# Dealing the rows of a repeated RMSNorm to partitions in sixteen groups of eight

## The chip, the core and the metric

The kernel runs on one core of a Trainium2 chip. The metric is the device time of one execution in microseconds (us), lower is better. The kernel before was timed three times: 238.52, 238.64 and 238.80 us, median 238.64 us.

## What is computed

The input x has 8 x 512 rows of 2,048 float32 numbers, 4,096 rows and 33.6 MB in all. Each row is written out twice, one copy after the other, and each copy is divided by the root of its mean square and multiplied by gamma. The output has 8,192 rows, 67.1 MB.

```python
def reference(x, gamma):
    B, S, D = x.shape
    x_rep = np.repeat(x, 2, axis=1)
    rms = np.sqrt((x_rep ** 2).mean(axis=-1, keepdims=True) + 1e-6)
    x_norm = x_rep / rms
    return (x_norm * gamma[None, None, :]).astype(np.float32)
```

Every row is treated by itself, so the row that a partition works on can be any row, as long as its two results are written where that row's results belong.

## The kernel before

The 4,096 rows are cut into four blocks of 1,024. In a block, SBUF partition p holds eight neighbouring rows: rows 8p to 8p + 7 of the block, 8 x 8,192 = 65,536 bytes in one piece. A block is brought in by one load (`load`, line 50): 128 partitions of 65,536 bytes, 8.39 MB. Its results, 16 rows for each partition, leave in two stores (`store`, line 53): h = 0 takes the results of the partition's first four rows, h = 1 those of the last four. Each store also moves 128 pieces of 65,536 bytes, 8.39 MB. So the kernel issues four loads and eight stores, all of one size, and all on the queue of SyncE (SP). In DRAM, the pieces of a load lie end to end (piece p + 1 begins where piece p ends); those of a store begin 131,072 bytes apart, because the other half's results lie between them.

All rows are held in one SBUF tensor `y` of 24 rows per partition, seen as three thirds of eight rows: `first`, `second` and `third`. The function `four` handles two blocks and is called twice (lines 128 and 129). It loads block n into the upper half of `first` and the lower half of `second` (line 92), and block n + 1 into `third` (line 94). Then, for each half block, ScalarE (ACT) squares the rows and sums them (`squares`, line 63) and takes the root of the mean (line 67); VectorE (DVE) forms the reciprocal (line 73) and multiplies each row by it and by gamma (`scale`, line 75); ScalarE or VectorE copies each result row to the row behind it (`repeat`, line 82); and the half is stored. Stores follow at lines 99, 103, 108 and 111.

The order of the work is written by hand. The SP queue works through loads and stores in the order in which they stand: two loads, four stores, and the same again in the second call. A load of the second call waits until the stores that read the same thirds have landed; each store waits for the copies that fill its third.

The two views of DRAM that the change touches are made at the top:

```python
    x_t = x.rearrange("b s d -> (b s) d").rearrange("(n p k) d -> n p k d", p=P, k=H * K)
    out_t = out.rearrange("b s d -> (b s) d").rearrange("(n p h j) d -> n h p (j d)", p=P, h=H, j=K * R)
```

P is 128, H is 2, K is 4 and R is 2. Gamma comes in by two small transfers on ScalarE's queue and is spread over the partitions by GpSimd (POOL).

Of the kernel before, what the change touches and what calls it, by code (L numbers as in the profile page):

```python
# [1 line left out]

# [4 lines left out]


@with_exitstack
def kernel(  # L10
    ctx: ExitStack,
    tc: tile.TileContext,
    x: bass.AP,
    gamma: bass.AP,
    out: bass.AP,
):
    nc = tc.nc
    P = nc.NUM_PARTITIONS
    f32 = mybir.dt.float32
    Act = mybir.ActivationFunctionType  # L20
    Alu = mybir.AluOpType

    B, S, D = x.shape
    Bo, So, Do = out.shape
    R = So // S
    assert R == 2 and D == Do and B == Bo and So == S * R
    eps = 1e-6
    inv_d = 1.0 / float(D)


    K = 4
    N = B * S
    ntiles = N // (P * K)
    assert N % (P * K) == 0 and ntiles == 8
    H = 2
    x_t = x.rearrange("b s d -> (b s) d").rearrange("(n p k) d -> n p k d", p=P, k=H * K)
    out_t = out.rearrange("b s d -> (b s) d").rearrange("(n p h j) d -> n h p (j d)", p=P, h=H, j=K * R)

    singles = ctx.enter_context(tc.tile_pool(name="singles", bufs=1))
    rows = ctx.enter_context(tc.tile_pool(name="rows", bufs=1))  # L40
    junk = ctx.enter_context(tc.tile_pool(name="junk", bufs=1, space=bass.MemoryType.PSUM))
    small = ctx.enter_context(tc.tile_pool(name="small", bufs=4))

    y = rows.tile([P, 3 * K * R, D], f32, name="y")
    first, second, third = 0, K * R, 2 * K * R

    def load(n, at):
        nc.sync.dma_start(out=y[:, at : at + H * K, :], in_=x_t[n])  # L50

    def store(n, h, to):
        nc.sync.dma_start(
            out=out_t[n, h], in_=y[:, to : to + K * R, :].rearrange("p j d -> p (j d)")
        )

    def squares(at, rows):

        n = len(rows)
        ss = small.tile([P, n], f32, name=f"ss{n}")  # L60
        for c, k in enumerate(rows):
            sq = junk.tile([P, D], f32, name="sq")
            nc.scalar.activation(  # L63
                out=sq[:], in_=y[:, at + k, :], func=Act.Square, accum_out=ss[:, c : c + 1]
            )
        rms = small.tile([P, n], f32, name=f"rms{n}")
        nc.scalar.activation(out=rms[:], in_=ss[:], func=Act.Sqrt, scale=inv_d, bias=eps_t[:])  # L67
        return rms

    def scale(at, to, rows, rms):  # L70
        n = len(rows)
        rstd = small.tile([P, n], f32, name=f"rstd{n}")
        nc.vector.reciprocal(out=rstd[:], in_=rms[:])  # L73
        for c, k in enumerate(rows):
            nc.vector.scalar_tensor_tensor(  # L75
                out=y[:, to + R * k, :], in0=y[:, at + k, :], scalar=rstd[:, c : c + 1],
                in1=gamma_b[:], op0=Alu.mult, op1=Alu.mult,
            )

    def repeat(to, k0, k1, copy):  # L80
        y_r = y[:, to + R * k0 : to + R * k1, :].rearrange("p (k r) d -> p k r d", r=R)
        copy(out=y_r[:, :, 1, :], in_=y_r[:, :, 0, :])  # L82

    ctx.enter_context(tc.manual_schedule())

    half = K // 2
    up, down = list(range(K)), list(range(K - 1, -1, -1))

    def four(n, constants):


        load(n, first + K)
        constants()
        load(n + 1, third)
        for rows in (up[:half], up[half:]):
            scale(first + K, first, rows, squares(first + K, rows))
        repeat(first, 0, half, nc.scalar.copy)
        repeat(first, half, K, nc.vector.tensor_copy)
        store(n, 0, first)
        scale(second, second, down, squares(second, down))  # L100
        repeat(second, half, K, nc.scalar.copy)
        repeat(second, 0, half, nc.vector.tensor_copy)
        store(n, 1, second)
        roots = [squares(third + h * K, up) for h in range(H)]
        scale(third, first, up, roots[0])
        repeat(first, 0, half, nc.scalar.copy)
        repeat(first, half, K, nc.scalar.copy)
        store(n + 1, 0, first)
        scale(third + K, third, up, roots[1])
        repeat(third, 0, K, nc.scalar.copy)  # L110
        store(n + 1, 1, third)

    gamma_b = singles.tile([P, D], f32, name="gamma_b")
    eps_t = singles.tile([P, 1], f32, name="eps_t")

    def constants():
        for c0 in (0, D // 2):
            nc.scalar.dma_start(
                out=gamma_b[0:1, c0 : c0 + D // 2],
                in_=gamma[c0 : c0 + D // 2].partition_broadcast(1),  # L120
            )
        nc.gpsimd.partition_broadcast(out_ap=gamma_b[:], in_ap=gamma_b[0:1, :])  # L122
        nc.vector.memset(eps_t, eps)  # L123

        root = singles.tile([P, 1], f32, name="root")
        nc.scalar.activation(out=root[:], in_=eps_t[:], func=Act.Sqrt)  # L126

    four(0, constants)
    four(2, lambda: None)


# [1 line left out]
_INS = ['x', 'gamma']  # L133
_OUTS = [((8, 1024, 2048), 'float32')]


# [23 lines left out]
```

## Time and profile before

| | |
|---|---|
| profiled execution, its own time | 238.68 us |
| its span (first to last record) | 236.7 us |
| median of the three timed runs | 238.64 us |
| ACT busy | 110.2 us, 47% of the span |
| DVE busy | 84.4 us, 36% |
| POOL busy | 2.5 us, 1% |
| moved by DMA | 100.68 MB in 1,733 packets, mean 425 GB/s |
| the SP queue's packets (q1) | 1,728: 1,536 of 65,536 bytes, and 192 that signal an end |
| one issue on the SP queue | 0.33 to 0.43 us |
| a load, from issue to landing | 39.2 us median |
| a store, from issue to landing | 24.8 us median |

A transfer is cut into packets, which sixteen DMA engines carry. The profile gives each packet's start, duration, size and queue, but not which of the sixteen engines carried it, nor which partition or address it served. The time from issue to landing contains the time in which a transfer stands behind earlier ones on the same sixteen engines. The duration of a single packet of 65,536 bytes in this execution is 2,418 ns in the median.

### The profile page before, as it was taken

What the parts mean: (1) busy time and instruction counts of PE and PEld (TensorE: products, weight loads), DVE (VectorE), ACT (ScalarE), POOL (GpSimd) and SP (SyncE); (2) the same over time, 40 slices, a digit from 0 to 9 for tenths busy, and PEclk for the clock granted to TensorE, in tenths of its full rate; (3) what the DMA queues carried; (4) which work ended last, traced back from release to release, by engine and by line L of the source; (5) the groups of instructions that cost most, each with busy time, mean ns of one, the idle gap of its engine ahead of it and who ended that gap; (6) DMA issues with size and microseconds to landing.
All of it is one profiled execution on the core that took longest, in us unless ns stands there. A gap on an engine that the chain in (4) does not pass through costs nothing.

```text
span 236.7 us, 218 instructions
## 1 busy us (share of the span) xinstructions
DVE 84.4 (36%) x47; ACT 110.2 (47%) x86; POOL 2.5 (1%) x5
## 2 busy tenths in 40 slices
DVE  0000495594699400000000008929909992000000
ACT  2001989479998460000000058991999947300000
POOL 0210000000000000000000000000000000000000
DMA  9898989999898989899898989899898989899894
GB/s 355 355 532 354 532 354 487 399 443 443 365 520 354 532 354 509 377 465 421 354 532 354 532 354 520 367 399 487 354 532 354 520 365 509 376 465 421 365 520 177
DMA packets 1733, 100.68 MB, mean 425 GB/s; under 512 B 194, under 2 KB 194, under 8 KB 196
## 3 DMA queue, kind: packets, MB, share of 16 engines
q1 hardware_dynamic: 1728, 100.66, 98.5%
q10 hardware_dynamic: 4, 0.01, 0.0%
q14 instruction: 1, 0.01, 0.0%
HBM read 33.56 MB, written 67.11 MB: 425 GB/s over the span
## 4 chain that ended last, share of the span: by engine, by line
DMA 45%; ACT 26%; DVE 13%; issue 1%; DVEq 0%; SPq 0%
DMA y<-in_x_dram 26%; DMA out_dram<-y 20%; ACT sq L63 15%; DVE y L75 13%; ACT y L82 11%; ACT rms L67 1%; DVE rstd L73 0%; DVEq L75 0%; SPq L50 0%
## 5 line engine op out<-in xcount | busy, mean ns | idle before, releaser
L63 ACT ACTIVATE sq<-y 128x2048 f32<-128x2048 f32 x32 | 60.1, 1878 | 72.0 <-DMA y<-in_x_dram 71.3
L75 DVE SCALAR_TENSOR_TENSOR y<-y,rstd,gamma_b 128x2048 f32<-128x2048 f32 x32 | 73.8, 2349 | 2.1 <-DMA out_dram<-y 1.5
L82 ACT COPY y<-y 128x4096 f32<-128x4096 f32 (+1 forms) x10 | 42.6, 4283 | 19.5 <-DVE y L75 19.5
L73 DVE RECIPROCAL rstd<-rms 128x4 f32<-128x4 f32 (+1 forms) x10 | 1.7, 170 | 109.0 <-ACT rms L67 109.0
L82 DVE COPY y<-y 128x4096 f32<-128x4096 f32 x4 | 9.2, 2293 | 0.1
L63 ACT ACTIVATION_READ_ACCUMULATOR sq<-y 128x1 f32 x32 | 6.0, 186 | 0.0
L67 ACT ACTIVATE rms<-ss,eps_t 128x4 f32<-128x4 f32 (+1 forms) x10 | 3.0, 297 | 0.3
L122 POOL PARTITION_BROADCAST gamma_b<-gamma_b x1 | 2.3, 2294 | 10.2 <-DMA gamma_b<-in_gamma_dram 10.2
L126 ACT ACT_TABLE_LOAD x1 | 1.3, 1283 | 1.5 <-PEq L144 1.5
L123 DVE MEMSET eps_t<- 128x1 f32 x1 | 0.1, 59 | 0.8 <-PEq L144 0.8
L126 ACT ACTIVATE root<-eps_t 128x1 f32<-128x1 f32 x1 | 0.2, 203 | 0.0
L144 POOL MEMSET const-bfloat16-1.0<- 128x1 bf16 x1 | 0.1, 103 | 0.0
L144 POOL MEMSET const-float32-0.0<- 128x1 f32 x1 | 0.1, 100 | 0.2 <-issue 0.2
L144 POOL MEMSET const-uint8-127<- 128x1 uint8 x1 | 0.1, 102 | 0.0
L144 POOL MEMSET const-float32-1.0<- 128x1 f32 x1 | 0.1, 99 | 0.0
## 6 DMA issues: line engine op xcount, KB each, us to landing
out_dram<-y SPq DMA_DIRECT2D x8, 24.8
y<-in_x_dram SPq DMA_DIRECT2D x4, 39.2
gamma_b<-in_gamma_dram ACTq DMA_DIRECT2D x2, 4.0 KB
```

The costliest lines, as they stand in the source:

```text
L63: nc.scalar.activation(out=sq[:], in_=y[:, at + k, :], func=Act.Square, accum_out=ss[:, c : c + 1])
L67: nc.scalar.activation(out=rms[:], in_=ss[:], func=Act.Sqrt, scale=inv_d, bias=eps_t[:])
L73: nc.vector.reciprocal(out=rstd[:], in_=rms[:])
L75: nc.vector.scalar_tensor_tensor(out=y[:, to + R * k, :], in0=y[:, at + k, :], scalar=rstd[:, c : c + 1], in1=gamma_b[:], op0=Alu.mult, op ...
L82: copy(out=y_r[:, :, 1, :], in_=y_r[:, :, 0, :])
L122: nc.gpsimd.partition_broadcast(out_ap=gamma_b[:], in_ap=gamma_b[0:1, :])
L123: nc.vector.memset(eps_t, eps)
L126: nc.scalar.activation(out=root[:], in_=eps_t[:], func=Act.Sqrt)
L144: nc = _bacc.Bacc("TRN2", target_bir_lowering=False, num_devices=1)
```

## The change

Both DRAM views are cut another way. The 128 partitions are thought of as sixteen groups (`e`) of eight (`r`), partition p = 8e + r. Before, partition p held piece p of the block. After, it holds piece 16r + e. So the eight partitions of one group hold pieces that are sixteen pieces apart, and the first partitions of the sixteen groups hold sixteen pieces that lie next to each other. The DRAM side of every load and store now counts in three dimensions, 16 groups, 8 pieces, 16,384 numbers, where it counted 128 pieces before; the SBUF side still counts 128 partitions of 16,384 numbers. The new helper `groups` names this SBUF side for both. Number, size and order of the transfers stay the same, and so do all instructions of ACT and DVE and all SBUF addresses.

```diff
-    x_t = x.rearrange("b s d -> (b s) d").rearrange("(n p k) d -> n p k d", p=P, k=H * K)
-    out_t = out.rearrange("b s d -> (b s) d").rearrange("(n p h j) d -> n h p (j d)", p=P, h=H, j=K * R)
+
+    E = 16
+    x_t = x.rearrange("b s d -> (b s) d").rearrange(
+        "(n r e k) d -> n e r (k d)", r=P // E, e=E, k=H * K
+    )
+    out_t = out.rearrange("b s d -> (b s) d").rearrange(
+        "(n r e h j) d -> n h e r (j d)", r=P // E, e=E, h=H, j=K * R
+    )
...
+    def groups(at):
+        return y[:, at : at + K * R, :].rearrange("p j d -> p (j d)")
+
     def load(n, at):
-        nc.sync.dma_start(out=y[:, at : at + H * K, :], in_=x_t[n])
+        nc.sync.dma_start(out=groups(at), in_=x_t[n])
 
     def store(n, h, to):
-        nc.sync.dma_start(
-            out=out_t[n, h], in_=y[:, to : to + K * R, :].rearrange("p j d -> p (j d)")
-        )
+        nc.sync.dma_start(out=out_t[n, h], in_=groups(to))
```

## The prediction

> **What bounds the kernel now.** I read the busy shares first, then the page's table of DMA queues, then its forty slices, then a table of equal stretches of time, and the chain of waits last.
>
> ```profile
> span 236.7 us, 218 instructions
> DVE 84.4 (36%) x47; ACT 110.2 (47%) x86; POOL 2.5 (1%) x5
> ...
> DMA  9898989999898989899898989899898989899894
> GB/s 355 355 532 354 532 354 487 399 443 443 365 520 354 532 354 509 377 465 421 354 532 354 532 354 520 367 399 487 354 532 354 520 365 509 376 465 421 365 520 177
> ...
> q1 hardware_dynamic: 1728, 100.66, 98.5%
> ...
> DMA y<-in_x_dram 26%; DMA out_dram<-y 20%; ACT sq L63 15%; DVE y L75 13%; ACT y L82 11%; ACT rms L67 1%; DVE rstd L73 0%; DVEq L75 0%; SPq L50 0%
> ```
>
> No compute engine is busy half of the time. The sixteen DMA engines are: the SP queue alone fills 98.5% of their span, 0.985 x 236.7 = 233.1 us for each. The swing between 354 and 532 GB/s is one of counting: a slice lasts 5.92 us, and 2 or 3 rounds of sixteen 65,536-byte packets (1.05 MB) end in it. The chain names compute for some 40% of the span, but that is work done while the queue still held earlier transfers; I don't price by it.
>
> Next, whether loads and stores run at one rate. Each transfer takes about 19.35 us, so stretches of 38.7 us hold two:
>
> ```profile
> core 0: us, DVE busy (x) ACT busy (x) POOL busy (x), PEclk, DMA share, GB/s
> 1.70:40.40 38.70, 11.85 (x7) 18.20 (x18) 2.29 (x1) 1.00 1.02 434
> 40.40:79.10 38.70, 29.52 (x16) 30.41 (x26) 0.00 (x0) 1.00 1.00 434
> 79.10:117.80 38.70, 0.81 (x1) 7.02 (x1) 0.00 (x0) 1.00 1.01 434
> 117.80:156.50 38.70, 11.85 (x7) 17.00 (x16) 0.00 (x0) 1.00 1.00 434
> ```
>
> The first stretch is two loads, the second two stores, and both move 434 GB/s, whatever ACT and DVE do beside them. A limit that differs between reading and writing DRAM would show here. What both directions share is the DMA engine and its way to SBUF. The packet records agree: of the 1,536 packets of 65,536 bytes all but 38 last within 22 ns of 2.418 us (27.1 GB/s each). The exceptions are fifteen in the first round (2.5 to 3.4 us), sixteen around 117 us, where the queue passes from stores to loads, and a few strays; together they exceed the floor by 0.96 us per engine. A lone 4,096-byte packet of gamma takes 0.156 us, 26 GB/s: one engine alone is as fast as one among sixteen. So the row reads as sixteen separate ways, each full, not as one shared total.
>
> The sum of the profiled execution: 1,536 / 16 = 96 packets x 2.418 = 232.1 us per engine; 0.96 us above the floor; 0.6 us of gaps between first and last packet; 3.0 us of span before and after; 2.0 us outside the span (238.68 against 236.7). That makes 238.7; the median of the runs is 238.64, so no correction is due.
>
> **The change, part by part.** It removes and adds no instruction: four loads and eight stores stay on the SP queue, at 0.33 to 0.43 us an issue, hidden behind the transfers already queued; a third counting dimension could lengthen these twelve issues, and while a transfer of 19.35 us stands in the queue that costs nothing (if the first issue alone doubled, 0.4 us would show). Squares, scales and copies read and write the same SBUF addresses with the same shapes: difference nothing. Were their cover gone, ACT's 110.2 us would have to show; it lies beside 233.1 us of transfers.
>
> Two things do move. One is the DRAM address at which the sixteen engines work at a time. Its most favourable price is the removal of all that stands above the floor: -0.96 us, and no more, since 1,498 packets already stand on 2.418. Its least favourable one is the first round's mean, about 3.05 us, for every packet: 96 x 0.63 = +60 us. I take 0, because 1,498 of the 1,536 rows are at the floor with either direction's address pattern.
>
> [...]
>
> The other is the dealing of partitions to engines. Before, both sides of a transfer counted 128; now DRAM counts 16 x 8 and SBUF 128. If each engine takes one of the sixteen, it serves eight neighbouring partitions, one after the other, and all engines step through their groups together. The trace of before shows neither which engine serves which partitions nor how the ways into SBUF are shared, so this is bounded from both sides. Below: every engine keeps a way of its own, 0 us. Above: engines meet in pairs, and two packets share what one had, 2 x 2.418 = 4.84 us a packet and +232.1 us on the whole. The ends lie far apart. The nearest rows are the two 434 GB/s stretches, which say that a way has nothing to spare: whatever sharing comes in is paid in full. I take sharing in pairs, less what the engines' offset saves. The sixteen end signals of one transfer come within 0.4 to 1.0 us, first to last, so two engines of a pair are 0.1 to 1.0 us apart. If they share a way for half a group (my assumption: four packets, 9.67 us at the floor) and then move on together, the earlier one is alone for that offset: 1% to 10% of the sharing goes, 209 to 230 us stay. At 5%: 0.95 x 232.1 = +220.5 us.
>
> [...]
>
> What is late next: all transfers stretch alike, so the waits of loads on stores and of stores on copies become shorter in proportion; ACT's and DVE's work, which fitted beside transfers of 19.35 us, fits beside longer ones. Gamma's second piece, late behind the first load's packets, is needed only after that load has landed. No new wait is added.
>
> **Sum.** 238.7 + 220.5 + 0 = 459 us.
>
> **Rivals.**
>
> 1. *Each engine keeps its own way* (the regrouping leaves the dealing of partitions as it was, or the ways aren't shared; then the change does to DRAM addresses alone what it says, or not even that). For it: 1,498 packets at one duration in both directions, and no sign of sharing anywhere. Against it: the two sides no longer count alike. Price -0.96 to +0.5 us: 237.7 to 239.2 us. Within it, the faster end needs half of the slow first rounds to go: 238.2 or less. This rival is the one that isn't slower.
>
> 2. *Pairs meet once and part.* If one engine of a pair is favoured, it gets four packets ahead, the other follows on the way that it left, and both are full from there. One wait of 4 x 2.418 = 9.7 us, 248 us; with a slow parting anything up to the forecast, so 248 to 400. For it: the spacing of the end signals repeats from transfer to transfer, so an offset once gained persists. Against: nothing in the rows favours an engine.
>
> 3. *DRAM decides.* Neighbouring pieces at a time collide, and packets last as in the first round: on the loads alone a third of 60 us, 259 us; on all, 299 us. For it: the slow rounds stand at the first load's start and where stores give way to loads. Against: they are over within two rounds, though the address pattern goes on.
>
> **How the numbers follow.** Forecast 0.58, rival 1 0.27, rival 2 0.10, rival 3 0.05. The forecast's own range is 400 to 472 us: up to full sharing (238.7 + 232.1 = 471) and a little, down to where a third of the sharing is gone. What the measurement can tell from no change is 0.2%, 0.48 us. Rival 1 splits into 0.16 faster and 0.11 within 0.2%. Slower has the rest, 0.73. To hold the time 8 times in 10 the range must reach from the forecast over rivals 2 and 3 to the unchanged part of rival 1: 238.1 to 474 us, which leaves out the faster 0.16 and a small tail. The cases of both signs are so far apart that nothing narrower would be honest.
>
> **What would show it.** Right: packets of 65,536 bytes near 4.8 us with some at 2.418 where a pair is apart; the SP queue's share still above 95%; the rate in a stretch near 220 GB/s for loads and stores alike; a transfer near 37 us; busy times of ACT and DVE as before. Rival 1: packets at 2.418 us, and only the first rounds differ. Rival 2: long packets at the start only. Rival 3: loads and stores at different rates. The forecast is wrong if loads stay near 434 GB/s in the first 40 us.

## The result, and the profile after

| | before | after |
|---|---|---|
| median | 238.68 us (4 runs, 238.52 to 238.80) | 450.86 us (4 runs, 447.69 to 452.09) |
| profiled execution, its span | 238.68 us, 236.7 us | 447.69 us, 445.6 us |
| a load, from issue to landing, median | 39.2 us | 79.7 us |
| a store, the same | 24.8 us | 73.1 us |

The changed kernel takes 1.886 times as long (95% interval 1.880 to 1.892). The forecast was 459 us, 1.9% above the median.

The page of the changed kernel, in the order in which the page of before was read (span, busy engines, DMA share and rate in forty slices, the SP queue):

```profile
span 445.6 us, 216 instructions
...
DVE 84.4 (19%) x47; ACT 110.8 (25%) x86; POOL 2.5 (1%) x5
...
DMA  9999999989999998999999999998999899999930
GB/s 189 212 259 188 188 188 212 353 188 200 241 218 224 229 224 224 218 247 277 194 253 224 224 200 212 224 229 300 282 265 300 224 253 282 224 247 247 253 100 24
...
q1 hardware_dynamic: 1728, 100.66, 95.9%
```

ACT and DVE are busy for as long as before, within 0.6 us. The number and the bytes of the packets are the same. The DMA engines are busy almost throughout, as before, and move half as much: the queue's share of 95.9% goes with a mean of 226 GB/s here, 98.5% went with 425 before. So a busy DMA share says that packets are under way, not that they are fast. Two stretches of 36 us, one in each of the first two loads (columns: window, its length, busy time of DVE, ACT and POOL, PE clock, DMA share, GB/s):

```profile
5.00:41.00 36.00, 0.00 (x0) 0.00 (x0) 2.29 (x1) 1.00 0.99 204
44.00:80.00 36.00, 23.55 (x13) 23.91 (x21) 0.00 (x0) 1.00 0.99 204
```

204 GB/s stand where 434 stood. The packet records say the same by single packets: 5.12 us in the median of the first load, 2.12 times the 2.418 us of before. Later in the run the rate is more often 220 to 300 GB/s, and there packets of all durations from 2.4 to 6.0 us occur. The end signals of the sixteen engines, which lie within 1.1 us in the two first loads, lie 12 us apart at the second call's first load and 25.5 us apart in the last store: engines drift apart. The last two slices of the DMA row (3 and 0 tenths) are the tail in which only some of them still have work.

The parts of the 447.7 us: 232.1 at the floor, 194.9 per engine above it, 15.1 of gaps (most of them that tail), and 5.6 around the transfers. Before, these were 232.1, 0.96, 0.64 and 5.0.

### The profile page after: what moved, and what is told of

Its sections match the earlier page's. It is cut to its first block, busy times and chain, and to the rows that moved or that the text cites. A ratio compares the mean times of both kernels' runs of the same rounds, so it can differ in the third digit from the quotient of the medians.

```text
span 445.6 us, 216 instructions
## 1 busy us (share of the span) xinstructions
DVE 84.4 (19%) x47; ACT 110.8 (25%) x86; POOL 2.5 (1%) x5
## 3 DMA queue, kind: packets, MB, share of 16 engines
q1 hardware_dynamic: 1728, 100.66, 95.9%
## 4 chain that ended last, share of the span: by engine, by line
another core or an unknown queue 44%; ACT 16%; DVE 13%; DMA 10%; issue 0%; DVEq 0%
DVE y L82 12%; DMA y<-in_x_dram 10%; ACT sq L70 9%; ACT y L89 6%; ACT rms L74 0%; DVE rstd L80 0%; DVEq L82 0%
## 5 line engine op out<-in xcount | busy, mean ns | idle before, releaser
L70 ACT ACTIVATE sq<-y 128x2048 f32<-128x2048 f32 x32 | 60.1, 1878 | 188.6 <-DMA y<-in_x_dram 187.9
L82 DVE SCALAR_TENSOR_TENSOR y<-y,rstd,gamma_b 128x2048 f32<-128x2048 f32 x32 | 73.8, 2348 | 49.9 <-DMA out_dram<-y 49.4
## 6 DMA issues: line engine op xcount, KB each, us to landing
out_dram<-y SPq DMA_DIRECT2D x8, 73.1
y<-in_x_dram SPq DMA_DIRECT2D x4, 79.7
```

Source lines behind the costliest of these rows:

```text
L70: nc.scalar.activation(out=sq[:], in_=y[:, at + k, :], func=Act.Square, accum_out=ss[:, c : c + 1])
L82: nc.vector.scalar_tensor_tensor(out=y[:, to + R * k, :], in0=y[:, at + k, :], scalar=rstd[:, c : c + 1], in1=gamma_b[:], op0=Alu.mult, op ...
```

## The experiments

Three theories were set against each other. *Dealing*: each engine serves one group of eight neighbouring partitions, and engines whose partitions lie 32 apart share a way into SBUF. *DRAM*: neighbouring runs, read or written at one time, collide. *The count*: a DRAM side in three dimensions costs by itself. All times below are medians, against the kernel before on the same chip (238.6 to 238.8 us).

### The same groups, far apart in DRAM

```diff
-        "(n r e k) d -> n e r (k d)", r=P // E, e=E, k=H * K
+        "(e n r k) d -> n e r (k d)", r=P // E, e=E, k=H * K
...
-        "(n r e h j) d -> n h e r (j d)", r=P // E, e=E, h=H, j=K * R
+        "(e n r h j) d -> n h e r (j d)", r=P // E, e=E, h=H, j=K * R
```

> Sixteen groups of eight as in the change, but each group's eight pieces lie end to end in DRAM and the groups 2 MiB apart (block n takes pieces 32e + 8n + r), so that no two engines are at neighbouring runs. Dealing theory (each engine serves eight neighbouring partitions and pairs of engines share a way into SBUF, wherever the DRAM addresses are): 440 to 460 us, packets again near 5.1 us in the first loads. DRAM theory (neighbouring runs at the same time collide): back near 239 us, packets 2.42 us.

Measured: 444.3 us in the median; three runs took 444.3 to 445.5 us, and one took 431.97, below the expectation. So 193 to 207 of the 212 us of loss are there. The packets of the first loads last 5.12 us again, and 5 to 41 us into the run 204 GB/s are moved, as in the changed kernel. Nothing is neighbouring here. The DRAM theory falls as the cause.

### 128 on both sides, other addresses

```diff
-    x_t = x.rearrange("b s d -> (b s) d").rearrange("(n p k) d -> n p k d", p=P, k=H * K)
+    x_t = x.rearrange("b s d -> (b s) d").rearrange("(p n k) d -> n p k d", p=P, k=H * K)
...
-    ... "(n p h j) d -> n h p (j d)" ...
+    ... "(p n h j) d -> n h p (j d)" ...
```

> DRAM is counted by 128 on both sides as before, but the blocks are interleaved: partition p of block n holds piece 4p + n, so pieces lie 256 KiB apart in a load and 512 KiB in a store instead of 64 and 128. Dealing theory: addresses don't matter, 238.2 to 239.5 us. DRAM theory: another address pattern gives another time, more than 2% away from 238.7.

Measured: 240.55 us, 1.0079 (1.0064 to 1.0094). That is between the two expectations: addresses do matter, by 1.9 us, but that is less than a hundredth of what the change cost. The packet records place the loss: 2.28 us per engine above the floor instead of 0.96, and the excess lies where stores give way to the loads of the second call, 110 to 130 us into the run.

### The loads alone, the stores alone

The edits are against the changed kernel. For the loads alone, `out_t` goes back to the count of before:

```diff
-        "(n r e h j) d -> n h e r (j d)", r=P // E, e=E, h=H, j=K * R
+        "(n p h j) d -> n h p (j d)", p=P, h=H, j=K * R
```

For the stores alone, `x_t` does:

```diff
-        "(n r e k) d -> n e r (k d)", r=P // E, e=E, k=H * K
+        "(n p k) d -> n p (k d)", p=P, k=H * K
```

> Only the loads are dealt in sixteen groups of eight; the stores keep the view of before, so the output rows stand in another order than the reference's. Dealing theory: four of twelve transfers take 5.12 instead of 2.42 us a packet: 4 x 8 x 2.70 = 86 us more, about 325 us, less what pairs that part save (from 300). If only writing to DRAM suffered: 239 us.

> Only the stores are dealt in sixteen groups of eight; the loads keep the view of before, so the output rows stand in another order than the reference's. Dealing theory: eight of twelve transfers are longer, up to 8 x 8 x 2.70 = 173 us more, 411 us at most; as pairs drift apart mainly in the stores, 350 to 411. The gains and losses of this and the loads-only run should add up to the 212 us of the change within some 30 us. If only loads suffered: 239 us.

Measured: loads alone 322.75 us, 1.352 (1.350 to 1.354), so +84.1 us for four loads, 21.0 each, where full sharing at 5.12 us gives 21.6. Stores alone 391.64 us, 1.636 (1.629 to 1.644), +153.0 us for eight, 19.1 each. Both directions pay. Together they make 237.1 us, and the change cost 212.2: some 25 us are saved when both are dealt so. The packet records place most of that in the stores of the second call: sorted by their starts, their packets exceed the floor by some 49 us per engine in the changed kernel and by some 70 in the stores-alone run. In the one, engines end the load before these stores 12 us apart; in the other, they end the first of these stores 1.3 us apart.

The end signals fit a store's paying less than a load. In the loads-alone run they stay within 1.1 to 2.4 us for the whole run. In the stores-alone run they lie 0.7 us apart in the last load ahead of the stores, then 3.3, 7.6, 11.9 and 17 us from one store to the next. So engines part in stores, and in the loads of the loads-alone run they hardly do. The changed kernel is less clear: there the spread also grew from 6.7 to 12 us in the second call's first load, which engines began while others were still at the store before it, and it stayed at 12 in the next load.

### Which partitions share a way

A kernel without arithmetic moves four partitions at a time, one packet for each of four engines, three transfers in a row; three packets of one engine make three rounds.

```python
        for at in (first, second, third):
            nc.sync.dma_start(
                out=part(at, K * R)[0 : 3 * step + 1 : step], in_=pieces[q : q + 4]
            )
...
    four_partitions(4, 0)
    four_partitions(32, 4)
    four_partitions(1, 8)
```

> No normalization is computed: only transfers of four partitions of 65,536 bytes, three at a time, four packets each. Loads into partitions 0, 4, 8, 12; then 0, 32, 64, 96; then 0, 1, 2, 3; then 0, 4, 8, 12 again; then stores from the same three sets. If a way into SBUF serves four neighbouring partitions and the four 32 higher: 2.42 us a packet for the first set, about 5.1 for the second (0 with 32, 64 with 96), about 10 for the third, in both directions. If every engine has its own way wherever it writes: 2.42 us in all.

After these loads come a second set with step 4 and stores from the same three sets. The windows of this kernel each hold two rounds, except the fourth, which holds four, and the last, which holds one. The first three are loads with steps 4, 32 and 1; the fourth is step 4, two rounds of loads and two of stores; the last two are stores with steps 32 and 1 (columns: window, length, POOL, PE clock, DMA share, GB/s):

```profile
core 0: us, POOL busy (x), PEclk, DMA share, GB/s
5.50:10.35 4.85, 0.00 (x0) 1.00 0.25 108
14.60:24.90 10.30, 0.00 (x0) 1.00 0.25 51
33.70:52.90 19.20, 0.00 (x0) 1.00 0.25 27
56.40:66.05 9.65, 0.00 (x0) 1.00 0.25 109
72.70:82.95 10.25, 0.00 (x0) 1.00 0.26 51
92.50:102.75 10.25, 0.00 (x0) 1.00 0.25 26
```

Four of sixteen engines are busy in every line (0.25 or 0.26). Four separate ways carry 108 GB/s, two carry 51, one carries 27 (26 in stores). Single packets: 2.418 us for step 4; 5.126 us for step 32; 9.64 us in loads and 10.21 us in stores for step 1. So partitions 0 to 3 are on one way. Partitions 0, 32, 64 and 96 are on two, for a packet took two packets' time and not four; this run doesn't show which two share. The load counted 4 x 8 (partitions 0 to 31) ran at 2.42 us, the one counted 5 x 8 (0 to 39) had one slow pair, and the one counted 8 x 8 (0 to 63) ran near 5.1 (all below), so the partners of 0 to 31 lie in 32 to 63. Read together, the runs make 0 share with 32.

### Which counts deal partitions badly

A kernel without arithmetic moves 128 partitions, one transfer after the other.

```python
    def dealt(view, e):
        return view.rearrange("(r e) c -> e r c", e=e)
```

> No normalization is computed: one 8.39 MB transfer after the other, each waiting for the last. Loads with DRAM counted by 128; 16 x 8; 32 x 4; 64 x 2; 8 x 16; 128; then a store by 128, a load by 128 and a store by 16 x 8. Dealing theory: the counts by 128 take 19.4 us and some 2 for start and end; 16 x 8, 32 x 4 and 64 x 2 deal eight neighbouring partitions to each engine and take about 41 us; 8 x 16 uses eight engines or as many ways and takes at least 39; the store as the load. DRAM theory: 16 x 8, 32 x 4 and 64 x 2 put different runs beside each other and differ by more than 10%.

The windows span, in order, the packets of the loads counted 128, 16 x 8, 32 x 4, 64 x 2 and 8 x 16, then of the stores counted 128 and 16 x 8:

```profile
core 0: us, POOL busy (x), PEclk, DMA share, GB/s
1.70:22.50 20.80, 0.00 (x0) 1.00 0.96 403
24.20:65.40 41.20, 0.00 (x0) 1.00 0.98 204
67.40:88.30 20.90, 0.00 (x0) 1.00 0.97 401
89.90:110.50 20.60, 0.00 (x0) 1.00 0.97 407
112.20:193.30 81.10, 0.00 (x0) 1.00 0.50 103
217.10:236.70 19.60, 0.00 (x0) 1.00 0.99 428
260.00:300.60 40.60, 0.00 (x0) 1.00 0.98 207
```

16 x 8 takes 41 us and 8 x 16 takes 81 us, on eight engines (share 0.50), both with packets near 5.1 us. But 32 x 4 and 64 x 2, which I expected at 41 us too, run like 128. In these loads three dimensions cost nothing in the transfer itself (401 and 407 GB/s, 403 for 128), so the theory of the count falls, and the dealing theory stands in a narrower form: the loss comes with an outer count of sixteen (or eight). By the theory an engine is then given whole groups of eight (or sixteen), while with 32 groups of four a group fits on one way; which engine is given what, no record shows. The narrower form was made after this run.

### Starting engines late

If a pair four packets apart never meets on one way, a late start of the right engines should cure the changed kernel.

```diff
+    def delay(engines, packets):
+        held = x.rearrange("b s d -> (b s) d").rearrange(
+            "(e n k) d -> e n (k d)", n=32, k=H * K
+        )
+        nc.sync.dma_start(out=groups(third)[0 : engines * packets], in_=held[0:engines, 0:packets])
...
+        if n == 0:
+            delay(12, 4)
+            delay(4, 4)
         load(n, first + K)
```

> The changed kernel with two small loads of x ahead of the first load, into rows that the second load overwrites: one on twelve engines, four packets each, one on four engines, four packets each. If the lower-numbered engines take them, engines 0 to 3 start 8 packets late, 4 to 11 four, 12 to 15 none, so that the pairs 0 and 4, 8 and 12 and so on are four packets apart. Dealing theory with pairs 32 partitions apart that share a way for half a group: they never meet, 8 extra packets, 8 x 2.42 = 19 us at most: 250 to 275 us. DRAM theory, or a cost of the three-dimensional count itself: some 450 us plus up to 20.

> The same with eight packets in place of four: the pairs stand a whole group apart and meet on the same way again, one transfer later. Dealing theory: 450 to 490 us (the extra packets at full or half speed), packets near 5.1 us. If any offset between engines were enough, whatever its size: 260 to 290 us.

Measured: 464.66 us, 1.946 (1.943 to 1.949), with four packets, and 520.05 us, 2.177 (2.173 to 2.181), with eight. The first missed the dealing theory's 250 to 275 us by far and lies where the other theories had it (450 to 470), which the runs above had ruled out; the second lies above its own. Part of this was the experiment. The SP queue's timeline (start, duration, issue) shows that the two small loads, which write the same rows, waited for each other:

```profile
0.72 23.74 SPq L100 DMA_DIRECT2D y<-in_x_dram  x2
24.51 22.39 SPq L59 DMA_DIRECT2D y<-in_x_dram  x2
```

The second was issued at 24 us, when the first was over, so only four engines started late. But even then, by the dealing theory, eight engines should have been free of each other, and all packets of the first load stayed near 5.07 us. In the stores, engines did part. Of the next two stretches, the first lies in the first load and the second in the stores after the loads (columns: window, its length, busy time of DVE, ACT and POOL, PE clock, DMA share, GB/s):

```profile
26.00:62.00 36.00, 0.00 (x0) 0.00 (x0) 0.00 (x0) 1.00 1.03 217
108.00:146.00 38.00, 12.87 (x7) 20.10 (x19) 0.00 (x0) 1.00 0.99 324
```

In the two loads none of 256 packets took less than 2.5 us; in the second stretch 120 of 188 did. Between 108 and 146 us the changed kernel has none. After 146 us the gain is gone: up to 300 us, it is 26 of 517.

So the run was repeated without arithmetic, with small loads that wait for nothing; in its first part four engines get four one-packet loads ahead of a load counted 16 x 8:

```python
    late(second, 4, 4, 4)
    load()
```

> No normalization is computed. Three loads of 128 partitions as 16 x 8, all into the same rows: the first behind four one-packet loads on four engines, the second behind four on twelve engines and four on four, the third behind nothing; then a store. The small loads go to rows of their own, so that nothing waits for them. Sharing in pairs alone, with the small loads on the lowest-numbered engines: in the first load half of the engines run at 2.42 us a packet after the start, 46 us in all; in the second load nearly all, 60 us in all with the small loads and 57 of 128 packets or more at 2.42; the third 41 us, all near 5.1. Theory that one pair slows the engines beside it: the first load stays near 5.1 throughout.

The windows are the first load while all engines work on it, its end, and the third load, which had nothing ahead of it:

```profile
core 0: us, POOL busy (x), PEclk, DMA share, GB/s
9.70:44.90 35.20, 0.00 (x0) 1.00 1.00 209
45.00:53.10 8.10, 0.00 (x0) 1.00 0.24 97
122.40:158.00 35.60, 0.00 (x0) 1.00 1.00 206
```

The late engines change nothing while the others work: 209 GB/s against 206, packets near 5.07 us. Only when twelve engines have finished, the last four run at 2.42 us. The expectation from sharing in pairs alone fell. The second load came while its small loads were still under way and is too mixed to show a cause; it missed its expectation as well, with 20 packets near 2.42 us, all at its end, where 57 or more were expected.

### Engines that are alone beside pairs

> No normalization is computed: loads one after the other. In order: 48 partitions as 12 x 4, DRAM pieces side by side; the same with groups 2 MiB apart; three loads of partitions 0, 4, ... 28 with pieces end to end; the same 2 MiB apart; three loads of partitions 0, 8, ... 40; 96 partitions as 12 x 8; 32 as 4 x 8; 64 as 8 x 8; a store. Sharing in pairs alone: 12 x 4 has 32 packets near 5.1 us and 16 of 2.42 us; the step of 8 has 12 near 5.1 and 6 of 2.42; 12 x 8 has 64 near 5.1 and 32 of 2.42; 4 x 8 all 2.42; 8 x 8 all 5.1; the distance in DRAM changes nothing. Theory that one pair on a shared way slows the engines beside it too: all packets of 12 x 4, 12 x 8 and the step of 8 near 5.1. DRAM theory for the late-engine runs: only the loads 2 MiB apart are slow.

Of the first theory's five counts those for 4 x 8 and 8 x 8 held, that for the step of 8 held in part, and those for 12 x 8 and 12 x 4 didn't. The second theory missed the step of 8. The packet records gave: 32 partitions as 4 x 8, 28 of 32 at 2.42 us and the first round near 3.3; 64 as 8 x 8, all slow; six single partitions 8 apart, two engines of which are alone, 4 of 18 at 2.42 to 2.47 us and their first two packets near 3.0. But 12 x 8 had none at 2.42 us, 93 of 96 above 4.5, and 12 x 4 had none either. The groups 2 MiB apart ran like those side by side, and eight single partitions 2 MiB apart at 2.42 us, so that distance isn't the reason.

> No normalization is computed. Loads one after the other, counted 16 x 8; 5 x 8; 6 x 8; three of twelve single partitions 0, 8, ... 88; 12 x 8; 16 x 8. Then stores one after the other, 16 x 8; 12 x 8; 5 x 8; and three of the twelve single partitions. In 5 x 8 the partitions of groups 0 and 4 lie 32 apart and three groups are alone; in 6 x 8 two pairs and two alone; in both twelves four pairs and four alone. If only pairs are slowed: the lone ones' packets at 2.42 us (24 of 40, 16 of 48, 12 of 36, 32 of 96). If any pair slows every engine of a load: all near 5.1 in each load. If engines that share a way upstream are slowed with the pair (engine numbers four apart): 5 x 8 and 6 x 8 keep their lone engines fast, both twelves are all slow. If it is the handing out of pieces within one transfer: 5 x 8, 6 x 8 and 12 x 8 all slow, the twelve single ones keep 12 fast. Stores: in the changed kernel's stores pairs drift apart and in its loads they don't, so lone engines should be fast in every store: 32 of 96, 24 of 40, 12 of 36 at 2.42.

The windows are the load counted 5 x 8, the load 12 x 8, the store 12 x 8 and the store 5 x 8:

```profile
core 0: us, POOL busy (x), PEclk, DMA share, GB/s
45.70:84.80 39.10, 0.00 (x0) 1.00 0.22 67
143.30:184.40 41.10, 0.00 (x0) 1.00 0.74 153
272.90:313.40 40.50, 0.00 (x0) 1.00 0.62 155
316.30:356.80 40.50, 0.00 (x0) 1.00 0.22 65
```

The share column tells who was done early. Twelve engines, eight of them in pairs to the end and four alone and done in half the time, make (8 + 4/2) / 16 = 0.62: the store. Twelve busy to the end make 0.75: the load. Five engines with one pair make (2 + 3/2) / 16 = 0.22: load and store alike. The packets agree: 28 of 96 at 2.42 us in the store 12 x 8 and none in the load, 21 of 40 in both directions of 5 x 8. So a single pair leaves the others alone, four pairs slow lone engines in a load, and in a store they don't. Of the expectations for loads, the one by which engines share a way upstream fits both; that they do isn't shown. The transfers of 6 x 8 and of twelve single partitions in this kernel overlapped, and nothing is read from them.

### Neighbouring runs without shared ways

```diff
-    E = 16
+    E = 32
```

> The changed kernel with 32 groups of four partitions in place of 16 of eight (E = 32): partition 4e + r holds piece 32r + e, so neighbouring runs of DRAM are still read and written at the same time. As the 32 x 4 load alone took 20.7 us: dealing theory 237.7 to 239.7 us, packets 2.42 us. If neighbouring runs in DRAM or the third dimension of the count cost anything, above 240; if they are worth what the change was for, at most 0.96 us below 238.7.

Measured: 240.62 us, 1.0080 (1.0066 to 1.0094), above the dealing theory's range by 0.9 us and in the range of a small cost of neighbouring runs or of the count. The packets stand at 2.42 us, and 210 us of the loss are gone with one number. What remains is 1.8 us. A part is the issue on the SP queue, here for the four loads of this kernel (minimum, median, maximum in ns):

```profile
L59 SPq DMA_DIRECT2D y<-in_x_dram x4: 583/592/667, 0.7 to 120.8; - x4
```

Before, it took 340 to 425 ns. Only the first one shows: the first packet starts at 2.22 us instead of 1.73, 0.5 us. The rest is 0.8 us per engine more above the floor, about half of it again where stores give way to loads, and 0.5 us of gaps. Of the forms that were run, none beat the kernel before.

## Why the prediction was right, and where a size was off

- *What bounds the kernel.* The transfers, 233.1 us at full ways. Right: packets make up 427.0 of the changed kernel's 447.7 us.
- *Dealing of partitions.* The step on which all hung, "If each engine takes one of the sixteen, it serves eight neighbouring partitions". No record names engines, so this is inferred, but closely: the 16 x 8 count halves the rate of a load with either order of DRAM addresses that was run (204 GB/s in both, where 434 stood), and partitions 32 apart share a way (5.126 us a packet, 2.418 alone).
- *The price of sharing.* That engines meet in pairs was my assumption, which no trace of before shows; afterwards four engines on partitions 0, 32, 64 and 96 moved 51 GB/s, and 108 on 0, 4, 8 and 12. I took 2 x 2.418 = 4.84 us a packet. Measured 5.12, 2.12 times: two packets on one way lose another 6%. Full sharing would then have added 96 x 2.70 = 259 us, not 232.
- *What the offset saves.* I took 5% of the sharing, from engines that keep an offset of 0.1 to 1.0 us. Measured 194.9 of 259 us remain, so 25% was saved, and the later ends gave 15.1 us of gaps back. The step that failed is "then move on together": the offset doesn't stay, it grows, mostly in the stores (1.1 us in the first loads, 6.7 in the fourth store, 25.5 in the last). The first error is worth 27 us, the second some 52 the other way, the gaps 14: the sum came out 11 us above the profiled execution and 8 above the median. The mechanism was right; that the sum lies within 2% is partly luck, since these errors cancel. The range's lower end was also called a third of the sharing gone; two thirds of 232.1 us make 393 us, not 400.
- *Rival 2, pairs that meet once and part.* Partly true. They part, but over eight stores and not at the first meeting, and never for good.
- *Rival 1, each engine keeps its way.* It holds for 32 x 4 (packets at 2.42 us) and not for 16 x 8 (5.12 us in the first loads).
- *Rival 3 and the DRAM term, taken as 0.* Not the cause. Its size is about 2 us: 1.9 in the 128 count with other addresses, 1.3 with neighbouring runs once the issue is taken off. It lay on the side of a loss, and -0.96 us was not to be had. Loads and stores did differ in rate, which was put down as this rival's sign (204 GB/s in the first loads, 231 from 125 to 222 us, in stores), but the sign can't tell it from pairs that part in stores. The 128 count with other addresses has pieces 256 KiB apart in loads and 512 KiB in stores, where 64 and 128 KiB stood, and that run lost 0.8%.
- *The third dimension in the issue.* I allowed 0.4 us for the first; it was 0.5.
- *What is late next.* No compute wait took over. ACT's wait for loads grew from 71.3 to 187.9 us and DVE's for stores from 1.5 to 49.4 us, but the DMA engines were busy meanwhile.

What stays open: why lone engines are slow in a load beside four pairs and not beside one. No run here shows which engines share what. That loads keep pairs together and stores let them part is seen in the end signals (1.1 to 2.4 us apart in the loads-alone run, up to 17 us in the stores-alone run) and in the run that starts engines late (no packet of 256 under 2.5 us in the loads, 120 of 188 in a stretch of stores); why they differ isn't shown. Whether the engines of E = 32 really are at neighbouring runs at one moment isn't in the records either.

## What to carry to other kernels

Where transfers fill the DMA engines, try the shape in which a transfer counts its outermost dimension: for 128 partitions, 128 on both sides was fastest here (238.6 us for the kernel, 240.6 with 32 x 4), a DRAM side split 32 x 4 or 64 x 2 as fast per packet (401 and 407 GB/s in a load, 403 for 128), and 16 x 8 half as fast (204). The number 32 alone is no rule: the store that ends the kernel with pairs beside lone engines, 32 partitions counted 32 on both sides, had packets of 4.97 to 5.13 us. Look at the duration of single packets, or GB/s beside the DMA share; a share near 1 hides a halved rate (0.99 at 204 GB/s here). And before rearranging addresses for locality, ask how far the packets are from their floor: here 0.96 us was all that could be won by it.

## What the runs showed of the hardware that I had not expected

- A DRAM side counted 32 x 4 or 64 x 2 loads 128 partitions as fast as one counted 128 (20.6 to 20.7 us), while 16 x 8 takes 41.1 and 8 x 16 takes 80.9.
- Two packets on one way cost more than a fair split, 5.126 us instead of 4.84, and so do four in stores, 10.21 us instead of 9.67; four in loads don't (9.64).
- Loads and stores differ under sharing: in a load of twelve engines with four pairs all packets were near 5.1 us, in the store of the same shape the four lone engines ran at 2.42.
- One issue on the SP queue takes 0.54 to 0.66 us in the changed kernel, with the third dimension, and 0.33 to 0.43 before, without it.
